# A two-layer diffusion trunk on one core: the modulation vectors are summed, biased and stored in another way, and their background steps are placed at other points

## The chip, the cores and the metric

The kernel runs on 1 core of one Trainium2 chip. The metric is the device time of the whole program in microseconds (us). The kernel before ran three times: 1853.0, 1855.58 and 1855.71 us, median 1855.58 us. The one execution that the profiler recorded took 1847.79 us.

## The reference, cut to what matters

The model has two layers over 512 latent tokens and 256 context tokens, each 1024 wide, in float32. Layer 0 mixes tokens by neighbourhood attention beside a spatial gating unit, layer 1 by a retention mixer. Each layer ends with a gated MLP that holds a depthwise convolution. Six modulation vectors per layer, the adaLN vectors, shift, scale and gate every sub-layer:

```python
silu_c = jax.nn.silu(c)
silu_cc = jax.nn.silu(c_ctx)
for i in range(DEPTH):                      # DEPTH = 2
    ctx_out = i < DEPTH - 1
    mod_lat = (silu_c @ ada_w[i] + ada_b[i])[:, None, :]
    mod_ctx = (silu_cc @ ada_w[i] + ada_b[i])[None, None, :]
    sh1, sc1, g1, sh2, sc2, g2 = jnp.split(mod_lat, 6, axis=-1)
    ...
    h_lat = modulate(rmsnorm(x, norm_g[i, 0]), sh1, sc1)      # x * (1 + scale) + shift
    ...                                                       # hybrid mixer or retention
    x = x + g1 * rmsnorm(y_lat, norm_g[i, 1])
    h = modulate(rmsnorm(x, norm_g[i, 2]), sh2, sc2)
    x = x + g2 * rmsnorm(conv_ffn(h, ...), norm_g[i, 3])
    ...                                                       # the same for the context, in layer 0
```

`ada_w` is 2 x 1024 x 6144 floats, 50 MB. The product with a single row (one for the latent tokens, one for the context) has very little arithmetic for each byte, and the change is about how the kernel computes it beside everything else.

## The kernel before, in words

**Stages.** The program goes through five stages in order: the spatial gating unit (`sgu`, from 0 to about 160 us of the span), the attention heads (`attention`, about 160 to 360, with the residual and norm that follow it to about 430), the MLP of layer 0 (`ffn(0)`, to about 935), the retention mixer (`retention`, to about 1475) and the MLP of layer 1 (`ffn(1)`, to the end). Float32 matmuls are made of three products of a high and a low part each (`mm3`); every weight block of 128 x 1024 floats (512 KB) is loaded by the SP queue into one of three buffers called `raw`, and `split` makes the high part on ACT and the low part on DVE.

**The background job.** Almost all adaLN vectors are computed in the background by `ada_half`, a Python generator. One half is 512 columns of one of the six vectors, so a layer has halves 0 to 11. Layer 0 computes halves 4 to 11 this way for two streams (latent and context), layer 1 halves 0 to 3 for two streams and 4 to 11 for one. For each half, four loads of 512 KB called `ar` go through the same three `raw` buffers as the weights; for each of the eight 128-row blocks and each stream DVE does `acc = raw * c + acc` over 128 x 512 elements, with `c` one scalar for each partition. So `acc` holds 128 partial sums for each column. Then `split` makes `ah` (ACT) and `al` (DVE) of it, and TensorE adds over the partitions: with a matrix of ones (`ag`) for the gate vectors, whose product with the norm weights `ngr` goes to a gate tile, or with a selector (`ac`) for shift and scale, whose result is copied (`arow`), transposed (`at`) and put into small tiles called `ab`. The MLP of layer 0 has no room for its gate in the on-chip memory, so there (`away`) the product goes out to DRAM.

**How the sum starts in the kernel before.** GpSimd (POOL) clears `acc`, and a load puts the bias row into its partition 0, before the eight DVE steps.

**Where the steps stand.** The generator stops at each `yield`. The main program calls `self.bg()` at chosen points, and each call runs the job to its next stop. The calls for the sgu stage stand in its two loops; `attention` has three in the first projection (`project_pair`, which fills `pq`, `px`, `pk`, `pv` and `py` for a pair of heads, from weights `wq`, `wk` and `wv`) and one at every second of its 42 tile steps; `ffn(0)` has two or three and one or two more in each iteration over `j`; `retention` runs four steps after head 0 and four in each later head. A tile step of `attention` does the scores of one tile (`s`, then `sc` on DVE and ACT) and, two steps later, the transposes (`pt`) and the product with the values (`o`). After each pair of heads `take_qk` splits the projections into `q`, `ka` and `kb`, and POOL copies a part of `kb`. In `retention` a head has projections `rk`, `rq`, `rkc`, its `v` and `g` products (`rn`), the output transposes (`rt`) and the output product (`wr`); the weights of head 1 are `rwk1`, `rwq1`, `rwv1` and those of the output `rwo`.

**What sets the order.** A scheduler places the instructions of each engine from its own estimate of their times; an instruction that is issued with `V.hold` on keeps its place in the program's order. Each engine runs its instructions strictly one after the other, and so does each DMA queue: an instruction that waits holds up all that stand behind it. DMAs with an addition (`accum_op`) are issued by POOL, which also issues the DMAs that add the MLP's partial results `yp` to `yd` or `yf` in DRAM.

Of the kernel before, what the change touches and what calls it, by code (L numbers as in the profile page):

```python
# [13 lines left out]
ALU = mybir.AluOpType  # L14
# [64 lines left out]
class Trunk:  # L79
# [171 lines left out]
    def ada_half(self, l, half, streams, gate=None, away=False, fine=False, side=False):  # L251
        S, V, T, G = self.S, self.V, self.T, self.G
        m, h = divmod(half, 2)
        acc = []
        for s in range(streams):
            t = (self.lp if s else self.bp).tile([P, 512], F32, name=f"acc{l}{half}{s}", tag=f"acc{s}", bufs=1)
            G.memset(t, 0.0)
            (G.dma_start if side else self.load)(t[0:1], self.a["adab_row"][l * 12 + half : l * 12 + half + 1])
            acc.append(t)
        for kp in range(4):  # L260
            raw = self.bp.tile([P, 1024], F32, name=f"ar{l}{half}{kp}", tag="raw", bufs=3)
            self.load(raw, self.ada_unit_src(l, half, kp))
            for kk in range(2):
                k = kp * 2 + kk
                for s in range(streams):
                    V.scalar_tensor_tensor(
                        out=acc[s],
                        in0=raw[:, kk * 512 : kk * 512 + 512],
                        scalar=self.cs[:, 8 * s + k : 8 * s + k + 1],
                        in1=acc[s],  # L270
                        op0=ALU.mult,
                        op1=ALU.add,
                    )
                if fine and kk == 0:
                    yield
            yield
        sp = []
        for s in range(streams):
            hi = self.t2k(f"ah{l}{half}{s}", F32R)
            lo = self.t2k(f"al{l}{half}{s}", F32R)  # L280
            self.split(hi, lo, acc[s])
            sp.append((hi, lo))
            if fine:
                yield
            if m in (2, 5):
                ps = self.ps(f"ag{l}{half}{s}", "C")
                T.matmul(ps, self.ones, hi, start=True, stop=False)
                T.matmul(ps, self.ones, lo, start=False, stop=True)
                ngr = self.t2k(f"ngr{l}{half}{s}")
                row = l * 4 + (1 if m == 2 else 3)  # L290
                src = self.a["norm_g"][row : row + 1, h * 512 : h * 512 + 512].broadcast_to([P, 512])
                (G.dma_start if side else self.load)(ngr, src)
                dst = gate[s][:, h * 512 : h * 512 + 512]
                if away:
                    V.tensor_tensor(out=ngr, in0=ps, in1=ngr, op=ALU.mult)
                    G.dma_start(dst, ngr)
                else:
                    V.tensor_tensor(out=dst, in0=ps, in1=ngr, op=ALU.mult)
        if m in (2, 5):
            return  # L300
        ps = self.ps(f"ac{l}{half}", "C")
        n = 2 * streams
        for i in range(n):
            T.matmul(ps[:2], self.sel[:, i // 2, :], sp[i // 2][i % 2], start=(i == 0), stop=(i == n - 1))
        row = self.t2k(f"arow{l}{half}")
        S.copy(row[:2], ps[:2])
        yield
        pt = self.ps(f"at{l}{half}", "C", (P, 4, 2))
        for i in range(4):
            T.transpose(pt[:, i, :], row[:2, i * P : (i + 1) * P], self.ident[:2, :2])  # L310
        ab = self.ab[l, 0 if m < 2 else 1]
        gi = (l * 2 + (0 if m < 2 else 1)) * 8 + h * 4
        for s in range(streams):
            if m in (0, 3):
                V.tensor_copy(ab[:, s, 1, h * 4 : h * 4 + 4], pt[:, :, s])
            else:
                V.scalar_tensor_tensor(
                    out=ab[:, s, 0, h * 4 : h * 4 + 4],
                    in0=pt[:, :, s],
                    scalar=1.0,  # L320
                    in1=self.ng[:, gi : gi + 4],
                    op0=ALU.add,
                    op1=ALU.mult,
                )
# [525 lines left out]
    def attention(self, y, final):  # L850
        a = self.a
        with ExitStack() as ctx:
# [11 lines left out]
            tiles = [(h, b) for h in range(8) for b in (0, 1, 2, 3, 4)]  # L864
            n, lag = len(tiles), 2
            fills = self.project_pair(0, pairs[0])
            for i, f in enumerate(fills):
                f()
                if i in (0, 2, 4):
                    self.bg()  # L870
            self.take_qk(0, pairs[0])
            fills = self.project_pair(1, pairs[1])
            toks = (4, 5, 0, 1, 2, 3)
            for i in range(n + lag):
                if i < n:
                    h, b = tiles[i]
                    j, step = divmod(i, 10)
                    pr = pairs[j]
                    if step == 0:
                        pr["at"] = [ap.tile([P, 768], F32R, name=f"at{x}{j}", tag=f"at{x}", bufs=4) for x in range(2)]  # L880
                        if j == 3:
                            A = (
                                [pairs[0]["at"], pairs[1]["at"]],
                                [self.unit(a["hyb_out"][f * P : (f + 1) * P], f"woa{f}", at=Q3) for f in (0, 1)],
                            )
                            fills = self.out_pieces(*A, y, toks[:1], False, None, "ata", "A")
                    if b == 0:
                        self.bias_tiles(h, heads[h])
                    self.score(h, b, pr, heads[h])
                if fills and i < n:  # L890
                    fills.pop(0)()
                if i < n and step == 7 and j < 3:
                    while fills:
                        fills.pop(0)()
                    self.take_qk(j + 1, pairs[j + 1])
                if i < n and step == 9 and j < 2:
                    fills = self.project_pair(j + 2, pairs[j + 2])
                if i >= lag:
                    h2, b2 = tiles[i - lag]
                    self.weigh(h2, b2, pairs[h2 // 2], heads[h2])  # L900
                if i < n and step == 3:
                    self.take_v(j, pr)
                if i % 2:
                    self.bg()
            self.bg_all()
            for f in fills:
                f()
# [199 lines left out]
    def retention(self, y, final):  # L1107
        S, V, T, G, a = self.S, self.V, self.T, self.G, self.a
        KS = float(np.float32(P) ** np.float32(-0.5))
        with ExitStack() as ctx:  # L1110
# [135 lines left out]
            def score(h, c):  # L1246
                d = hd[h]
                ps = self.ps(f"rs{h}{c}", "B", (P, 2, 256))
                sd = self.t2k(f"sd{h}{c}", shape=(P, 2, 256))
                for i in range(2):  # L1250
                    kt = slice((2 * c + i) * P, (2 * c + i + 1) * P)
                    self.mm3(ps[:, i], [x[:, kt] for x in d["k"]], [x[:, 256 * c : 256 * c + 256] for x in d["q"]], True, True)
                for i in range(2):
                    dm = d["dl"][:, 128 - i * P : 384 - i * P]
                    V.tensor_tensor(out=sd[:, i], in0=ps[:, i], in1=dm, op=ALU.mult)
                s2 = d[c] = [rp.tile([P, 2, 256], F32R, name=f"sd{i}{h}{c}", tag=f"sd{i}", bufs=2) for i in range(2)]
                self.split(s2[0], s2[1], sd)
# [84 lines left out]
            for h in range(8):  # L1342
                vg_tiles(h)
                if h == 0:
                    x = [rp.tile([P, 1024], F32R, name=f"wx{i}", tag=f"kd{i}", bufs=1) for i in range(2)]
                    wv = [w8(self.ready[f"rwv0{i}"]) for i in range(2)]
                    wk = self.ready["rwk0"]
# [12 lines left out]
                    for half in range(2):  # L1360
# [6 lines left out]
                        for n in (range(4) if half else (2, 0, 1, 3)):  # L1367
# [10 lines left out]
                            if half and n == 2:  # L1378
# [1 line left out]
                                score(h, 0)  # L1380
                                score(h, 1)
                                states(h)
                    V.hold = True
                    self.bg(4)
                    V.hold = False
                else:
                    psk = self.ps(f"rk{h}", "A")
                    self.proj_t(psk, wk, 0)
# [13 lines left out]
                    for tp in (2, 0, 1):  # L1402
                        nat(h, wv, tp, "v")
                        if tp < 2:
                            score(h, tp)
                    self.bg()
                    wg = vg(h, 16, "g")
                    states(h)
                    for tp in range(2):
                        nat(h, wg, tp, "g")  # L1410
                    self.bg()
                if h < 7:
                    wk = qk(h + 1, 8, "k")
                else:
                    self.turn += 3
                    o6 = f, w_out(6)
                    self.bg_all()
# [13 lines left out]
    def ffn(self, l, y, final, gates=None):  # L1431
# [13 lines left out]
        with ExitStack() as ctx:  # L1445
# [241 lines left out]
            def o(i):  # L1687
                for _ in range(per[i]):
                    if pieces:
                        pieces.pop(0)()  # L1690
# [4 lines left out]
            for j in range(2, NF):  # L1695
# [20 lines left out]
                meet(pre, 0, 0, Z, ALU.add)  # L1716
                step()
                o(1)
                if j % 2 == 0 and group < LAST:
                    wo = nwo + [w_out(group + 1)]  # L1720
                    pieces += out_steps(feats, wo, group)
# [13 lines left out]
                o(3)  # L1735
                gs[j] = conv(j, pre)
                if j > 3:
                    self.bg(2 if first and j > 5 and j % 2 else 1)
            while pieces:
                o(0)  # L1740
            self.bg_all()
# [225 lines left out]
```

## Time and profile before

| what | before |
|---|---|
| median of three runs | 1855.58 us |
| the profiled execution | 1847.79 us, of which the span of the instructions is 1845.9 us |
| TensorE (PE) busy | 1777.3 us, 96% of the span |
| VectorE (DVE) busy | 1398.2 us, 76% |
| ScalarE (ACT) busy | 1030.1 us, 56% |
| GpSimd (POOL) busy | 331.1 us, 18% |
| the DVE steps of the background sums | 256 instructions, 185.3 us |

PE is the engine that is nearly always busy, so time is gained or lost where PE waits. A row of the waits names the waiting engine and tile and what it waited for, with the total, the number of times and the longest. A row of the timeline has start, length, engine, line, operation, tiles and number of instructions; brackets show how long the engine had been idle before it and what ended that. A row of the windows has the stretch, its length, and for each engine its busy time with its number of instructions, then the mean granted TensorE clock (1.00 is full speed), the share of time that the DMA engines were busy, and GB/s. Nearly all instructions carry one line number (L71, a helper that records them), so the tiles' names tell what an instruction is.

### The profile page before, as it was taken

To read this page: it belongs to the slowest core of one execution; us is meant where nothing else is said; L and a number is where in the kernel's file an instruction comes from. 1 tells how busy PE (TensorE), PEld (TensorE's weight loads), DVE (VectorE), ACT (ScalarE), POOL (GpSimd) and SP (SyncE) were. 2 spreads that over 40 slices of the span, in tenths; PEclk is the share of its full clock that TensorE was granted. 3 is DMA by queue.
4 is the path that set the end of the run, shared out by engine and by line. 5 is a ranking of instruction groups with operands and counts; after the bars stand their busy time and mean duration, and the time that the engine had idled before them with its cause. 6 is when DMAs were issued, how large, how long until landed. Compare 5 with 4: busy or idle time off the path is not lost. (4 is left out here: it accounts for less than half of the span.)

```text
span 1845.9 us, 28788 instructions
## 1 busy us (share of the span) xinstructions
PE 1777.3 (96%) x10928; PEld 1579.5 (86%) x10928; DVE 1398.2 (76%) x2359; ACT 1030.1 (56%) x1866; POOL 331.1 (18%) x462
## 2 busy tenths in 40 slices
PE   7999899999999999999999999999999889999997
PEld 4888777679998899998788989988999789999996
DVE  4877775789878788788867676676556699998887
ACT  6533555677565565565664534344334477766763
POOL 1102122131122322222112011011101100222221
PEclk9999999999999999999999999999999989999999
DMA  8344321155577777787622422331321225887762
GB/s 297 113 141 143 117 86 41 46 179 149 172 153 169 174 182 158 157 173 166 249 97 92 143 98 81 126 106 58 112 69 58 94 83 160 220 204 196 172 161 97
DMA packets 84399, 253.45 MB, mean 137 GB/s; under 512 B 11026, under 2 KB 11538, under 8 KB 84260
## 3 DMA queue, kind: packets, MB, share of 16 engines
q1 hardware_dynamic: 55044, 191.27, 31.3%
q0 software_dynamic: 26912, 51.95, 16.4%
q10 hardware_dynamic: 2304, 8.39, 1.1%
q8 instruction: 86, 1.41, 0.3%
q14 instruction: 53, 0.43, 0.1%
HBM read 191.80 MB, written 39.85 MB: 125 GB/s over the span
## 5 line engine op out<-in xcount | busy, mean ns | idle before, releaser
L71 DVE SCALAR_TENSOR_TENSOR acc<-ar,cs,acc 128x512 f32<-128x512 f32 x256 | 185.3, 749 | 29.4 <-DMA ar<-in_adaw 19.8
L71 DVE SCALAR_TENSOR_TENSOR cv<-pre,cw,cv 128x769 f32<-128x769 f32 (+1 forms) x176 | 153.2, 881 | 5.3 <-ACT cv L71 4.8
L71 PE MATMUL rn<-rwv,h0c 128*128 128x256 f32 x768 | 136.2, 281 | 2.9 <-ACT h0c L71 2.9
L71 PEld LDWEIGHTS rn<-rwv,h0c 128*128 128x128 f32 x768 | 118.1, 191 | 3.6 <-ACT h0c L71 3.3
L71 PE MATMUL wf<-fo,g 128*128 128x512 f32 x432 | 112.4, 394 | 0.1
L71 PE MATMUL rn<-rwv,h1c 128*128 128x256 f32 x384 | 108.1, 282 | 0.4 <-DVE h1c L71 0.2
L1680 POOL DMA_DIRECT2D yf<-yp x64 | 55.1, 861 | 254.4 <-ACT yp L71 231.1
L71 ACT ACTIVATE cv<-pre,cw 128x770 f32<-128x770 f32 (+1 forms) x88 | 81.3, 925 | 22.2 <-DVE pre L71 21.6
L71 PE MATMUL rn<-rwg,h0c 128*128 128x256 f32 x512 | 89.8, 279 | 0.0
L71 PEld LDWEIGHTS wf<-fo,g 128*128 128x128 f32 x432 | 76.0, 188 | 13.0 <-DVE fo L71 0.5
L71 PE MATMUL px<-hs,wc 128*128 128x384 f32 (+1 forms) x480 | 78.4, 311 | 5.1 <-ACT pre L71 2.7
L71 PEld LDWEIGHTS px<-hs,wc 128*128 128x128 f32 x480 | 73.8, 190 | 10.1 <-ACT pre L71 4.3
L71 ACT COPY yp<-wf 128x512 f32<-128x512 f32 x118 | 67.8, 576 | 21.6 <-PE wf L71 18.5
L71 ACT ACTIVATE pre<-px 128x256 f32<-128x256 f32 (+2 forms) x160 | 54.2, 366 | 44.2 <-PE px L71 44.0
L71 PEld LDWEIGHTS rn<-rwg,h0c 128*128 128x128 f32 x512 | 78.0, 189 | 0.0
L71 PE MATMUL pz<-hb,wa 128*128 128x384 f32 (+1 forms) x480 | 77.4, 308 | 0.0
L71 PE MATMUL px<-hb,wa 128*128 128x384 f32 (+1 forms) x480 | 77.2, 308 | 0.0
L71 PE MATMUL py<-blk,wb 128*128 128x384 f32 (+1 forms) x480 | 76.9, 308 | 0.0
L71 PE MATMUL px<-blk,wb 128*128 128x384 f32 (+1 forms) x480 | 76.7, 308 | 0.0
L71 PEld LDWEIGHTS px<-hb,wa 128*128 128x128 f32 x480 | 73.3, 188 | 3.2
L71 PEld LDWEIGHTS px<-blk,wb 128*128 128x128 f32 x480 | 73.2, 188 | 3.0 <-ACT pre L71 0.2
L71 PEld LDWEIGHTS rn<-rwv,h1c 128*128 128x128 f32 x384 | 72.8, 190 | 1.5 <-DVE h1c L71 1.4
(1279 smaller groups left out, 5113.6 us busy)
## 6 DMA issues: line engine op xcount, KB each, us to landing
ar<-in_adaw SPq DMA_DIRECT2D x96, 512.0 KB, 3.9
yf<-yp POOLq DMA_DIRECT2D x64, 256.0 KB, 4.4
yd<-yp POOLq DMA_DIRECT2D x54, 256.0 KB, 4.9
yd<-ypg POOLq DMA_DIRECT2D x54, 256.0 KB, 4.9
fin<-xd SPq DMA_DIRECT2D x8, 512.0 KB
xn<-in_x SPq DMA_DIRECT2D x6, 512.0 KB, 4.9
xb<-in_x SPq DMA_DIRECT2D x6, 512.0 KB
xd<-xb ACTq DMA_DIRECT2D x6, 512.0 KB, 3.1
```

What stands on the lines that cost most here:

```text
L71: i = f(*args, **kw)
L1680: G.dma_start((yd[t] if first else y[t])[:, o], v, accum_op=ALU.add)
```

## The change

The sums no longer start from a cleared tile: the first DVE step writes `raw * c` (one `tensor_scalar`), and the seven others add as before. The bias row is added to partition 0 by an accumulating DMA of POOL's queue, issued after the last step of the sum. In the MLP of layer 0 the gate product is written into the tile of the sum, and goes to DRAM from there. The generator stops at one more place, after the last stream's split (for the gates after each stream's). The calls of `bg` stand elsewhere: none in the first projection of `attention` and then four in five tile steps from the fourth on, with the DVE order held; in `ffn(0)` four in each iteration; in `retention` the weight `rwk1` is asked for ahead of the steps after head 0, of which there are two and not four, and later heads have one step more.

```diff
@@ ada_half
         for s in range(streams):
             t = (self.lp if s else self.bp).tile([P, 512], F32, name=f"acc{l}{half}{s}", tag=f"acc{s}", bufs=1)
-            G.memset(t, 0.0)
-            (G.dma_start if side else self.load)(t[0:1], self.a["adab_row"][l * 12 + half : l * 12 + half + 1])
             acc.append(t)
...
                 for s in range(streams):
-                    V.scalar_tensor_tensor(
-                        out=acc[s],
-                        in0=raw[:, kk * 512 : kk * 512 + 512],
-                        scalar=self.cs[:, 8 * s + k : 8 * s + k + 1],
-                        in1=acc[s],
-                        op0=ALU.mult,
-                        op1=ALU.add,
-                    )
+                    w, c = raw[:, kk * 512 : kk * 512 + 512], self.cs[:, 8 * s + k : 8 * s + k + 1]
+                    if k == 0:
+                        V.tensor_scalar(out=acc[s], in0=w, scalar1=c, scalar2=None, op0=ALU.mult)
+                    else:
+                        V.scalar_tensor_tensor(out=acc[s], in0=w, scalar=c, in1=acc[s], op0=ALU.mult, op1=ALU.add)
                 if fine and kk == 0:
                     yield
+            if kp == 3:
+                for s in range(streams):
+                    row = self.a["adab_row"][l * 12 + half : l * 12 + half + 1]
+                    G.dma_start(acc[s][0:1], row, accum_op=ALU.add)
             yield
...
             self.split(hi, lo, acc[s])
             sp.append((hi, lo))
-            if fine:
+            if fine or m in (2, 5) or s == streams - 1:
                 yield
...
                 if away:
-                    V.tensor_tensor(out=ngr, in0=ps, in1=ngr, op=ALU.mult)
-                    G.dma_start(dst, ngr)
+                    V.tensor_tensor(out=acc[s], in0=ps, in1=ngr, op=ALU.mult)
+                    G.dma_start(dst, acc[s])
@@ attention
             fills = self.project_pair(0, pairs[0])
-            for i, f in enumerate(fills):
+            for f in fills:
                 f()
-                if i in (0, 2, 4):
-                    self.bg()
...
-                if i % 2:
+                if i > 2 and i % 5 != 2:
+                    self.V.hold = True
                     self.bg()
+                    self.V.hold = False
@@ retention, head 0
-                    V.hold = True
-                    self.bg(4)
-                    V.hold = False
+                    wk = qk(1, 8, "k")
+                    self.bg(2)
@@ retention, later heads
                         if tp < 2:
                             score(h, tp)
+                        if tp < 1:
+                            self.bg()
                     self.bg()
...
-                if h < 7:
+                if 0 < h < 7:
                     wk = qk(h + 1, 8, "k")
-                else:
+                elif h:
@@ ffn
                 o(1)
+                if first and j > 3:
+                    self.bg()
...
                 if j > 3:
-                    self.bg(2 if first and j > 5 and j % 2 else 1)
+                    self.bg()
```

## The prediction

> **What bounds the kernel now.** I read the busy times first, then the windows by stage, then the waits of PE, and last the timeline at the two places where the order of the background steps changes most. The page:
>
> ```profile
> PE 1777.3 (96%) x10928; PEld 1579.5 (86%) x10928; DVE 1398.2 (76%) x2359; ACT 1030.1 (56%) x1866; POOL 331.1 (18%) x462
> ...
> L71 DVE SCALAR_TENSOR_TENSOR acc<-ar,cs,acc 128x512 f32<-128x512 f32 x256 | 185.3, 749 | 29.4 <-DMA ar<-in_adaw 19.8
> ...
> ar<-in_adaw SPq DMA_DIRECT2D x96, 512.0 KB, 3.9
> ```
>
> PE is busy for 96% of 1845.9 us, so at most 68.6 us can be had without less PE work, and this change takes none away. The windows say where PE stands still:
>
> ```profile
> core 0: us, PE busy (x) PEld busy (x) DVE busy (x) ACT busy (x) POOL busy (x), PEclk, DMA share, GB/s
> ...
> 160.00:205.00 45.00, 38.90 (x217) 33.57 (x217) 31.59 (x51) 16.34 (x31) 15.73 (x17) 0.92 0.50 154
> 205.00:350.00 145.00, 143.53 (x831) 109.75 (x830) 101.30 (x293) 90.85 (x216) 31.17 (x46) 1.00 0.19 60
> ...
> 438.00:850.00 412.00, 406.88 (x2121) 375.84 (x2121) 336.25 (x478) 239.66 (x413) 99.81 (x130) 1.00 0.72 166
> 850.00:905.00 55.00, 50.12 (x262) 44.88 (x261) 49.90 (x72) 33.86 (x56) 5.74 (x7) 1.00 0.77 239
> ...
> 985.00:1030.00 45.00, 39.60 (x224) 33.08 (x223) 33.41 (x59) 22.60 (x34) 10.15 (x9) 1.00 0.41 138
> 1030.00:1450.00 420.00, 416.53 (x2958) 384.82 (x2958) 264.54 (x465) 175.11 (x251) 40.02 (x56) 1.00 0.28 93
> ```
>
> Idle of PE: 6.1 us in 160 to 205 (45.00 less 38.90, at a granted clock of 0.92), 1.5 in 205 to 350, 5.1 in 438 to 850, 4.9 in 850 to 905, 5.4 in 985 to 1030, 3.5 in 1030 to 1450. So there is something to win in three short windows, and in the attention loop (205 to 350) next to nothing to win and much to lose. The waits of PE over the first stretch and over 850 to 1080:
>
> ```profile
> PE s L71 <- POOL kb L962: 6.1, 1, 6.1
> ```
>
> ```profile
> PE rkc L71 <- ACT rwk L71: 2.1, 1, 2.1
> PE at L71 <- ACT arow L71: 2.0, 1, 2.0
> PE rt L71 <- DVE rg L71: 1.9, 2, 1.6
> PE wf0A L71 <- DVE fin L71: 1.7, 1, 1.7
> ...
> PE ag L71 <- ACT ah L71: 1.1, 1, 1.1
> ```
>
> **The operations themselves.** Of the 256 DVE steps, 32 become `tensor_scalar`.
>
> ```profile
> L71 DVE TENSOR_SCALAR sc<-sc,sst 128x512 f32<-128x512 f32 x30 | 15.0, 499 | 0.7
> ...
> L71 DVE CUSTOM_DVE_ANT_0 sc<-s,tm 128x256 f32<-128x256 f32 x30 | 12.6, 420 | 18.1 <-PE s L71 17.9
> L71 DVE SCALAR_TENSOR_TENSOR acc<-ar,cs,acc 128x512 f32<-128x512 f32 x17 | 12.5, 758 | 0.1
> ...
> L71 DVE RECIPROCAL sst<-sst 128x1 f32<-128x1 f32 x30 | 4.8, 161 | 9.3 <-ACT sc L71 8.8
> ...
> L71 DVE TENSOR_TENSOR at<-o,at 64x512 fp32r<-64x512 f32 x7 | 4.8, 683 | 5.5 <-ACT at L71 5.5
> ```
>
> DVE saves 32 x (749 - 499 ns) = 8.0 us. I put them at nothing: DVE is busy for 76%, and PE covers it; only where DVE is nearly full (attention, below) do they count, and they are in that term.
>
> ```profile
> L257 POOL MEMSET acc<- x32: 524/527/983, 0.9 to 1617.3; 128x512 f32 x32
> L71 ACT ACTIVATE ah<-acc x32: 614/632/640, 94.6 to 1677.2; 128x512 fp32r<-128x512 f32 x32
> ...
> L97 SPq DMA_DIRECT2D acc<-in_adab_row x18: 228/244/303, 51.9 to 1309.5; - x18
> L258 POOL DMA_DIRECT2D acc<-in_adab_row x14: 504/526/850, 282.1 to 1618.1; - x14
> ```
>
> POOL loses 32 x 0.53 = 16.9 us of clearing and gains 18 issues of 0.53 us; at 18% busy neither is on the path. SP loses 18 issues of 0.24 us: nothing. The gate product written to the tile of the sum has the same shape on the same engine: nothing. What is new is that `ah` on ACT can start only when the row DMA has landed behind the last DVE step. Before, the row landed long before:
>
> ```profile
> DMA to landing us min/median/max: 1.7/3.3/6.3
> ```
>
> So between the last step of a sum and its split stand 0.5 us of issue and 1.7 to 6.3 us of landing. POOL waits too, for the last step: behind it on POOL stand the `kb` copies and table loads in attention and the `yd` additions in the MLP. Price from both sides: nothing where the program gives the split later than that (retention, where the split stands some 45 us behind), and up to 6.8 us of ACT for each split where it follows at once. The price is part of the terms by stage.
>
> **160 to 205 us.** The timeline, DVE and then PE:
>
> ```profile
> 168.83 5.79 DVE L71 SCALAR_TENSOR_TENSOR acc<-ar,cs,acc 128x512 f32<-128x512 f32 x8
> ...
> 187.42 0.75 DVE L71 SCALAR_TENSOR_TENSOR acc<-ar,cs,acc 128x512 f32<-128x512 f32 x1 [5.20 <-DMA ar<-in_adaw]
> 188.20 0.42 DVE L71 TENSOR_TENSOR kb<-px,ka 64x256 fp32r<-64x256 f32 x1
> ```
>
> ```profile
> 191.56 0.63 PE L71 MATMUL pq<-h0a,wq 128*128 128x512 f32 x1
> ...
> 198.05 0.28 PE L71 MATMUL s<-ka,q 128*128 128x256 f32 x1
> ```
>
> ```profile
> 1075.47 5.48 PE rq L71 x24
> ```
>
> DVE stands for 5.20 us before a background step whose load is late; the `kb` split stands behind it, POOL copies it, PE waits 6.1 us. In the order of the changed kernel no background step stands there. The first scores then wait for nothing that I can see. Behind the stall the 24 `pq` matmuls take 6.49 us (198.05 less 191.56); 24 matmuls of that kind in retention take 5.48: about 0.9 us, from -0.1 to -3.1 (the whole window at 0.92), goes with the stall. Term: -6.1 - 0.9 = -7.0.
>
> **Attention, the weights of the last pair.** Halves 6 to 9 move some 50 to 80 us later, into the loop. All of `ar` and the weights share three buffers, on SP's queue. The weight `wq3r` takes the buffer of the second `ar` load of half 8, so it waits for the last DVE step on that.
>
> ```profile
> 245.76 0.35 SPq L97 DMA_DIRECT2D wq3r<-in_hyb_qkv  x1
> ```
>
> ```profile
> 276.70 0.68 DVE L71 TENSOR_TENSOR at<-o,at 64x512 fp32r<-64x512 f32 x1 [0.78 <-ACT at L71]
> ```
>
> ```profile
> 279.65 1.09 PE L71 MATMUL pt<-ident,sc 128*128 128x128 f32 x8
> ```
>
> ```profile
> L71 ACT ACTIVATE wq<-wq3r x1: 1059/1059/1059, 249.4 to 249.4; 128x1024 fp32r<-128x1024 f32 x1
> L71 DVE TENSOR_TENSOR wq<-wq3r,wq x1: 1222/1222/1222, 254.5 to 254.5; 128x1024 fp32r<-128x1024 f32 x1
> ```
>
> That step and three before it now stand right behind the DVE row at 276.70: 277.4 + 4 x 0.75 = 280.4. The load lands 3.9 later (284.3), ACT has the high part at 285.4, DVE the low part at 286.6. PE reaches `pq` of this pair behind the `pt` matmuls, at 280.7: a stall of 4.7 us (high part only) to 5.9 (both); I take the middle, 5.3, and 0.8 of clock as after the stall of 6.1. Bounds 0 (the DVE step runs earlier than it stood in time) to 8. The three other weights behind it on SP are asked for in turn, and come in the shadow of this stall. Term: +6.1.
>
> **Attention, the rest of 205 to 350.** DVE gets 52 steps of the sum where it had 17: 35 x 0.758 = 26.5, with two more splits 1.4, less four `tensor_scalar` 1.0: 101.3 becomes 128 of 145 us. The rows above show 18.1 + 9.3 + 5.5 = 32.9 us in which DVE waits in the softmax chain for PE and ACT. The steps stand with held order, so they fill such a wait only where they happen to stand. If u of the 32.9 stay unfilled, the window takes 128 + u. With the four splits waiting on ACT for row DMAs (ACT is at 63%) I take u = 20: +3; bounds 0 and +16. Without them moving, nothing would change here.
>
> **The MLP of layer 0.** Halves 10, 11 and the gates run 17 to 58 us earlier. In 438 to 850 PE idles only 5.1 us of 412, and one split can hold ACT for one landing: +1 (-2 to +4). In 850 to 905 the background is over before the stage's end; `at` (2.0) and a part of the wait for `fin` (1.7), whose load stands behind `ar` loads, go: -2.5 (-4 to 0).
>
> **Retention.** `rwk1r` is asked for ahead of the next half's loads, some 40 us earlier:
>
> ```profile
> 990.86 4.39 DMA rwk1r<-in_ret_qk
> ```
>
> It arrived at 995.3 and PE waited 2.1 for it; with `rt` (1.9) and `ag` (1.1) I take 5.0 of the 5.4 idle us as gone (0 to -5.4). Later heads have their halves 23 to 35 us later: -0.5 of 3.5.
> In the sgu stage no bias row is loaded ahead of its weights: -1.0 (-2 to +1). MLP of layer 1: nothing.
>
> **The sum.** -7.0 + 6.1 + 3 + 1 - 2.5 - 5.0 - 0.5 - 1.0 = -5.9. The profiled execution took 1847.79 us, so the changed kernel would take 1841.9 beside it. The median of the runs is 1855.58, 7.8 above that execution, so on its scale 1849.7, which I round to 1849.5. Its own range is 1842 to 1852.
>
> **The rivals.**
> 1. *The pair of weights comes in time and the loop hides the rest:* the terms +6.1 and +3 go, -15.0, 1840.6. For it: PE's idle there is 1.5 us, and DVE steps may run ahead of where they stood. Against it: one queue and three buffers.
> 2. *The late windows do not give:* with only the first stall gone, -7.0 + 6.1 + 3 + 1 = +3.1, 1858.7. A wait that ends is taken by the next (`rg`, `fin`), which have other causes than the background job. No change that can be measured, 0.2% being 3.7 us.
> 3. *DVE becomes the bound in the attention loop,* slower: held order leaves the 32.9 us unfilled, so the window takes 161 and not 145: +16 in place of +3, sum +7.1, 1862.7. It decides from u = 26 on, where the sum is 0. For it: PE cannot run on without `sc`, and every step between costs 0.75 us. Against it: tile steps run two ahead.
> 4. *ACT waits for the accumulating DMA,* slower: eight splits in the loop at 3.3 to 6.3 us, 26 to 50, of which half on the path: 19 in the middle in place of 3, sum +10.1, 1865.7. It decides from a landing of 2.2 us on if each is waited for in full. Against it: ACT has 54 us free here, and the split mostly stands some steps behind the DMA.
> The Trainium skill speaks against the change here. "SBUF — State Buffer", section "A bandwidth-pool intuition that's wrong (but worth ruling out)", has a GpSimd DMA at some 620 ns alone and 3100 ns beside a DVE copy that holds the shared port, since GpSimd then cannot write descriptors; as an estimate, eight times 3.1 is 25 us on ACT, half of it 12.4, and the sum would be +3.5. "DMA: Bandwidth & Descriptors" of the Trainium skill, section "Anatomy of one DMA — SWDGE (gpsimd) path", puts about 2.0 us on each such DMA: an estimate of 16 us, half of it 8, and the sum -0.9. The median landing of 3.3 us lies near the first, the least of 1.7 below the second; no row here tells which DVE instruction ran beside a landing.
>
> **How the numbers follow.** Forecast 0.43, rival 1 0.10 (both faster), rival 2 0.15 (same), rival 3 0.20, rival 4 0.12 (slower): 0.53, 0.15, 0.32. The range goes from 1839 to 1864, which leaves out about half of rivals 1, 3 and 4, 0.2 in all.
>
> **What would show it.** Right: no wait of `s` for `kb` near 185; `kb` split at once; a PE wait of about 5 us at the first `pq` of the last pair; no wait of `rkc` for `rwk`. Wrong: waits of PE for `sc` or `ptall` that sum to over 10 us between 205 and 350 (rival 3); ACT idle behind the row's landing ahead of `ah` over 3 us in most of 32 splits (rival 4); a new wait after `fin` or `rg` of the same length (rival 2). The prediction fails most easily if the held steps stand at the wrong place in the softmax chain.

## The result, and the profile after

The changed kernel took 1876.44 us (median of four runs, 1872.28 to 1877.65) against 1855.22 us before on the same chip: the ratio is 1.0117, with a 95% interval of 1.0103 to 1.0130, so it is 21 us slower. The forecast was 1849.5 us, 6 us faster. Its profiled execution took 1877.65 us.

The page of the changed kernel, busy times and the group of the background's sums:

```profile
PE 1791.7 (96%) x10928; PEld 1587.9 (85%) x10928; DVE 1389.4 (74%) x2359; ACT 1028.2 (55%) x1866; POOL 336.7 (18%) x448
...
L71 DVE SCALAR_TENSOR_TENSOR acc<-ar,cs,acc 128x512 f32<-128x512 f32 x224 | 161.9, 751 | 25.7 <-DMA ar<-in_adaw 24.9
```

DVE lost 8.8 us of work (1398.2 before), as the 32 cheaper first steps promised, and the program did not get shorter: PE's share of the span is again 96%, of a longer span. The windows of the changed kernel follow, with the columns of the prediction's windows. From the third row on, the bounds are shifted so that each holds about the same PE work as before; the first is the same stretch of time and holds more of it (262 matmuls for 217), the second a little less (811 for 831):

```profile
160.00:205.00 45.00, 45.00 (x262) 39.49 (x261) 17.91 (x39) 18.85 (x36) 13.51 (x18) 1.00 0.27 89
205.00:372.00 167.00, 149.60 (x811) 111.08 (x811) 124.36 (x324) 92.17 (x215) 43.63 (x47) 0.96 0.25 77
...
460.00:885.00 425.00, 413.26 (x2130) 378.82 (x2129) 344.69 (x498) 244.78 (x423) 99.05 (x122) 0.99 0.72 166
885.00:935.00 50.00, 48.46 (x252) 43.33 (x251) 38.54 (x53) 28.41 (x48) 5.25 (x6) 1.00 0.74 219
...
1015.00:1056.00 41.00, 40.76 (x240) 35.09 (x239) 27.04 (x49) 21.86 (x35) 6.73 (x9) 1.00 0.26 82
1056.00:1477.00 421.00, 417.40 (x2953) 386.30 (x2953) 263.95 (x469) 170.31 (x247) 41.39 (x56) 1.00 0.29 93
```

The stall at 184 is gone (PE is busy for all 45 us), the idle time around 1000 is gone (41 us where 45 were needed), and what is won there is lost twice over in two places: the attention loop, where PE now idles 17 us at a clock of 0.96, and the MLP of layer 0, where it idles 12 in place of 5.

To put numbers on the stages, each matmul of the changed kernel was paired with the same matmul of before (same tiles, same count) and the growth of its delay was read off over each stage. The column "again" is a second profile of the kernel before, taken on another chip, paired in the same way: it shows how far one program drifts.

| stage, in times of before | forecast | changed kernel | before, again |
|---|---|---|---|
| 0 to 180, gating unit and first projection | -1.0 | +3.0 | +1.6 |
| 180 to 205 | -7.0 | -9.1 | +2.4 |
| 205 to 350, attention loop | +9.1 | +27.8 | +0.1 |
| 350 to 440 | 0 | 0 | 0 |
| 440 to 850, MLP of layer 0 | +1 | +12.7 | -1.3 |
| 850 to 905, its end | -2.5 | -4.9 | +4.8 |
| 905 to 1030, retention, first heads | -5.0 | -4.7 | +2.3 |
| 1030 to 1450, later heads | -0.5 | +1.6 | +2.6 |
| 1450 to the end | 0 | +2.4 | +2.6 |

The columns of the two profiles add up to 29 and 15 us. The two profiled executions are 29.9 us apart (1877.65 and 1847.79); the one of before lies 7.4 below its median and the one of the changed kernel 1.2 above, which leaves the measured 21. Single values under some 5 us count only where they recur.

### The profile page after: what moved, and what is told of

Read it like the earlier page. It is cut to its first block, busy times and chain, and to the rows that moved or that the text cites. A ratio compares the mean times of both kernels' runs of the same rounds, so it can differ in the third digit from the quotient of the medians.

```text
span 1875.6 us, 28757 instructions
## 1 busy us (share of the span) xinstructions
PE 1791.7 (96%) x10928; PEld 1587.9 (85%) x10928; DVE 1389.4 (74%) x2359; ACT 1028.2 (55%) x1866; POOL 336.7 (18%) x448
## 5 line engine op out<-in xcount | busy, mean ns | idle before, releaser
L71 DVE SCALAR_TENSOR_TENSOR acc<-ar,cs,acc 128x512 f32<-128x512 f32 x224 | 161.9, 751 | 25.7 <-DMA ar<-in_adaw 24.9
```

The source lines that it names most:

```text
L71: i = f(*args, **kw)
```

## The experiments

Two theories stood at first. A: what costs is the accumulating DMA, since ACT, and DVE and PE behind it, wait for its landing. B: what costs is the new placement. Ratios are to runs of the kernel before on the same chip, with 95% intervals.

**One part undone or done alone.** The first run keeps all placements and puts the old start of the sums back.

```diff
+            G.memset(t, 0.0)
+            (G.dma_start if side else self.load)(t[0:1], self.a["adab_row"][...])
...
-                    if k == 0:
-                        V.tensor_scalar(out=acc[s], in0=w, scalar1=c, scalar2=None, op0=ALU.mult)
...
-                    G.dma_start(acc[s][0:1], row, accum_op=ALU.add)
```

> The changed kernel with one part undone: every sum starts again from a cleared tile with the bias row loaded ahead of it; all placements stay new. Theory A (the accumulating DMA: ACT stands behind its landing ahead of ah, and DVE and PE behind ACT): ACT's nine waits of 18.4 us go, the stall of PE at 214 us (4.9) with its 3.4 of clock goes, so about 1876 - 14 = 1862. Theory B (the placement alone: the three buffers and the held DVE order in attention): at most 3 us, 1873 to 1877, with the stalls of PE at 214 and at 284 unchanged.

Measured: 1.0046 (1.0027 to 1.0066), 8.6 us slower than before, so 13 us of the 21 go with the old start, near theory A's forecast. The second run does the reverse: the kernel before with only the new start (`tensor_scalar` and the accumulating DMA in, clearing and early row load out).

> The kernel before with one part of the change: the sums start with a scaled copy and the bias row comes by the accumulating DMA; the gates, the stops and all placements stay as before. Theory A: ACT waits at ah in the first projection and in the attention loop, 8 to 15 us slower than before, 1863 to 1870. Theory B: 1855 to 1858.

Measured: 1.0017 (0.9997 to 1.0036). With the old placements the new start costs 3 us, not clear of none, which was theory B's forecast. So neither part explains the loss alone; the two do it together. Where it costs, the timeline of the changed kernel shows; first at 97 us, in the gating unit:

```profile
96.96 1.82 POOL L274 DMA_DIRECT2D acc<-in_adab_row  x2 [8.78 <-DVE acc L71]
...
101.31 1.30 ACT L71 ACTIVATE ah<-acc 128x512 fp32r<-128x512 f32 x2 [4.23 <-DMA acc<-in_adab_row]
...
101.97 0.69 DVE L71 TENSOR_TENSOR al<-acc,ah 128x512 fp32r<-128x512 f32 x1 [4.66 <-ACT ah L71]
...
102.93 0.47 PE L71 MATMUL mx<-vnh,sguw 128*128 128x384 f32 x1 [1.86 <-ACT un L71]
```

ACT stands 4.23 us for the landing, and the activation `un` that PE needs stands behind it. By 160 to 180 us the three kernels with the new start and the old calls in the first projection (this one and two below) are 8.0 to 9.1 us late, the second profile of before 1.6. Then in the attention loop, at 214:

```profile
207.21 0.63 POOL L982 DMA_DIRECT2D slab<-in_rpb  x1 [0.30 <-POOL tm L996]
211.59 0.40 POOL L989 TENSOR_SCALAR slab<-slab 128x256 f32<-128x256 f32 x1 [3.75 <-DMA slab<-in_rpb]
212.11 1.68 POOL L274 DMA_DIRECT2D acc<-in_adab_row  x2
...
214.23 0.63 ACT L71 ACTIVATE ah<-acc 128x512 fp32r<-128x512 f32 x1 [2.81 <-DMA acc<-in_adab_row]
...
214.90 0.69 DVE L71 TENSOR_TENSOR al<-acc,ah 128x512 fp32r<-128x512 f32 x1 [2.50 <-ACT ah L71]
...
219.74 1.97 PE L71 MATMUL o<-ptall,vn 128*64 128x512 f32 x2 [4.92 <-ACT ptall L71]
```

The last step of the sum ended on DVE at 208.8, but the row DMA is issued only at 212.1: POOL stood 3.75 us for a table load ahead of it. Then come the landing, the ACT split, and behind that split, with other work of ACT between, the copy `ptall` that PE waits for. A wait on one queue became a wait on three engines. Over the whole of the changed kernel there are nine such waits of ACT, 18.4 us in all:

```profile
ACT ah L71 <- DMA acc<-in_adab_row: 18.4, 9, 4.2
```

**The attention placement.** The changed kernel with the old calls there:

```diff
-                if i > 2 and i % 5 != 2:
-                    self.V.hold = True
-                    self.bg()
-                    self.V.hold = False
+                if i % 2:
+                    self.bg()
```
(and the three calls in the first projection, and no added stop for these halves).

> The changed kernel with the attention placement (calls, held order, the new stop for these halves) as before; the start of the sums and the other placements stay new. Theory B: the stall of s for kb at 184 comes back (+8.5), those at 214 (8.3), at 284 to 292 (11.3) and around 330 (6.5) go: 1876 - 18 = 1858. Theory A: the accumulating DMA costs as much at the old places, some 1868.

Measured: 1.0044 (1.0028 to 1.0059), 8.2 us slower than before, between the two forecasts. The loop from 205 to 350 is as short as before and the stall at 184 is back, so the placement loses 13 us on balance. Next, the stall that the prediction had worked out, at 284 in the changed kernel:

```profile
282.91 0.33 SPq L97 DMA_DIRECT2D wq3r<-in_hyb_qkv  x1
...
286.45 1.06 ACT L71 ACTIVATE wq<-wq3r 128x1024 fp32r<-128x1024 f32 x1 [1.58 <-DMA wq3r<-in_hyb_qkv]
...
287.56 0.80 PE L71 MATMUL pq<-h0a,wq 128*128 128x512 f32 x1 [3.63 <-ACT wq L71]
```

Is this queue the bound of the loop (theory C), or DVE and its held order (theory D)? One run lets the weights pass two background loads, the other drops the held order.

```diff
-                if i > 2 and i % 5 != 2:
+                if i > 2 and i % 5 != 2 and not 14 < i < 20:
```

> The changed kernel without the background calls of tile steps 15 to 19, so that the three weights of the last pair are asked for two background loads earlier (the steps left out follow behind the loop). Theory C (three shared buffers on one queue): the wait of pq for wq near 284 (3.6) goes and with it the 8.7 to 11 us that the trace shows between 278 and 292; 10 us faster than the changed kernel, 10 to 12 slower than before. Theory D (DVE is full, with steps held in the softmax chain): the time moves to other waits in the loop, within 3 us of the changed kernel (20 slower than before).

```diff
-                    self.V.hold = True
                     self.bg()
-                    self.V.hold = False
```
(and, as in the run with the old calls above, no added stop for the halves that run up to the end of attention).

> The changed kernel without the held order of the background's DVE steps in the attention loop. Theory D: the scheduler may move the steps into the waits of the softmax chain, 8 us or more faster than the changed kernel. Theory C: the stall near 284 stays, within 3 us of the changed kernel (20 slower than before).

Measured: 1.0146 (1.0126 to 1.0165) for the first, 27 us slower than before, more than the change itself; 1.0049 (1.0030 to 1.0068) for the second, 9 us slower, so dropping the held order together with the added stop gives back 12 us. In the first run the stall at 284 is gone (from 220 to 300 nothing is lost), and some 25 us are lost between 305 and 345, mostly in waits for `sc` and `vt`. The steps left out did not leave the loop: all 52 still stand in it, 16 of them in its last 45 us, where the changed kernel has 7. So the run shows that the weights in time do not make the loop short, and theory C falls as its only bound; but it also crowded the steps at the loop's end, and what the weights alone would have given is not shown.

Is it the held order itself? The kernel before with the held order at its old calls:

```diff
                 if i % 2:
+                    self.V.hold = True
                     self.bg()
+                    self.V.hold = False
```

> The kernel before with one edit: the background's DVE steps in the attention loop keep their place in the program's order, at the old calls (17 steps of the sums there). If held order costs by itself, the loop from 205 to 350 loses 5 us or more against the kernel before. If it costs only with 52 steps in the loop, the loop loses at most 2 us and the time is that of before.

Measured: 0.9986 (0.9969 to 1.0003), the same time as before. The loop lost 7 us and the stretch to 205 gained 4. By the forecast that is held order costing by itself; but 28 steps stood in the loop where 17 had, so this run does not separate the order from the number of steps. So I counted, for every kernel, the DVE steps of the sums in the stretch that holds the same PE work (205 to 350 before). Two of these stretches, of the changed kernel and of the one without the held order; first the groups and the window of the changed kernel:

```profile
L71 DVE SCALAR_TENSOR_TENSOR acc<-ar,cs,acc 128x512 f32<-128x512 f32 x46 | 32.9, 763 | 0.0
L71 DVE TENSOR_SCALAR acc<-ar,cs 128x512 f32<-128x512 f32 x6 | 2.6, 477 | 0.0
```

```profile
199.00:372.00 173.00, 155.60 (x850) 116.52 (x850) 125.49 (x329) 93.58 (x218) 45.04 (x48) 0.96 0.24 75
```

and those without the held order:

```profile
L71 DVE SCALAR_TENSOR_TENSOR acc<-ar,cs,acc 128x512 f32<-128x512 f32 x22 | 17.3, 827 | 2.7 <-DMA ar<-in_adaw 2.7
L71 DVE TENSOR_SCALAR acc<-ar,cs 128x512 f32<-128x512 f32 x2 | 1.0, 476 | 0.0
```

```profile
210.00:359.00 149.00, 144.86 (x838) 110.31 (x836) 105.82 (x295) 90.01 (x214) 35.60 (x44) 1.00 0.22 66
```

| kernel | steps in the loop | held | length of the loop, us |
|---|---|---|---|
| new start alone, old calls in attention, the two kept parts (below), before again | 16 | no | 145 |
| before | 17 | no | 145 |
| one call less in the projection (below) | 20 | no | 147 |
| two calls less (below) | 24 | no | 150 |
| the change without held order | 24 | no | 149 |
| the same with the old start (below) | 27 | no | 153 |
| before with held order | 28 | yes | 152 |
| the change with the old start | 52 | yes | 165 |
| the change | 52 | yes | 173 |
| the change with the gap | 52 | yes | 177 |

The length goes with the number of steps, with the flag or without it: 27 steps without it make 153 us, 28 with it 152. No run changes the flag and keeps the number. From 17 to 52 steps with the old start the loop grows by 20 / 35 = 0.57 us for each, against 0.75 us that a step lasts. The window of that kernel, the change with the old start, shows it best, since no accumulating DMA stands in it:

```profile
192.00:357.00 165.00, 151.80 (x851) 114.78 (x850) 128.90 (x328) 93.12 (x218) 40.20 (x50) 0.98 0.26 78
```

DVE has 27.6 us more work than before (128.90 for 101.30), and the loop is 20 us longer. Before, DVE had 43.7 us without work in the loop; only 7.6 of them were filled, 36.1 are left, and DVE is busy for 78%. PE's waits for `sc` sum to 7.5 us there (the longest 3.9), and no step waits for a load. In the changed kernel DVE is busy for 125.49 of 173 us, 73%: it is not full, and yet the steps lengthen the loop.

For the kernels without held order the number of steps is not the whole cause. Much of what they lose falls at one place near 210, where DVE stands before a step whose load is late, as in the stall at 184. The kernel with 27 steps:

```profile
204.89 1.41 DVE L71 SCALAR_TENSOR_TENSOR acc<-ar,cs,acc 128x512 f32<-128x512 f32 x2 [2.13 <-DMA ar<-in_adaw]
```

```profile
210.03 0.69 PE L71 MATMUL vn<-ident,vt 128*128 128x128 f32 x2 [4.41 <-ACT ptall L71]
```

By 220 it has lost 6.6 of its 8 us; with two calls less it is 3.9 of 5. What these rows would lose without the late load is not shown.

So the change costs what it does in the loop because 52 steps stand there; without held order (and without the added stop) the scheduler leaves 24 and puts the others ahead. The accumulating DMA adds 8 us to that (173 against 165).

**The MLP of layer 0.** In every kernel with the new calls the stretch from 440 to 850 loses 10.5 to 13.2 us, whatever the start of the sums (13.2 with the old start). With the old calls it loses less than 1, or gains 3 with the new start. Two theories. E: too many steps in an iteration. F: the added step stands ahead of the request for the output weights `fo` on SP's queue; ACT's waits for `fo` sum to 12 us in the changed kernel and 6 before. One run puts the second step at the end of each iteration, in a kernel with the retention part and the new start kept (see below), the other moves the step behind the request for `fo`, in the changed kernel with the old attention.

```diff
-                    self.bg(2 if first and j > 5 and j % 2 else 1)
+                    self.bg(2 if first else 1)
```

> The same two kept parts, old attention, and in the MLP of layer 0 two steps at the end of every iteration from j = 4 on (before: two only in odd iterations from j = 7): as many steps in each iteration as the change has, but none ahead of the request for the output weights fo. Theory E (too many steps in an iteration: DVE and ACT are late for the convolution): the MLP of layer 0 loses 8 to 13 us between 440 and 850, so 3 to 8 slower than before. Theory F (the added step asks for its 512 KB ahead of fo on SP's queue, so fo lands late): at most 3 us lost there, 3 to 6 faster than before.

```diff
                 o(1)
-                if first and j > 3:
-                    self.bg()
...
                 o(2)
                 if j % 2 and j - 1 < LAST:
                     nwo = [w_out(j - 1)]
                 if first and j > 3:
-                    self.bg()
+                    self.bg(2)
```

> The changed kernel with the old attention placement (8.2 us slower than before in its run) and one more edit: the step added in each iteration of the MLP of layer 0 is called after the request for fo and not ahead of it, so that the same number of steps stands in each iteration. Theory F: ACT's waits for fo (some 12 us) and with them 6 to 10 of the 10.5 us between 440 and 850 go; equal to before within 3 us. Theory E: nothing changes, 8 us slower than before.

Measured: 1.0003 (0.9989 to 1.0018) for the first, 0.6 us slower than before and 6 slower than the same kernel without the edit; its stretch from 440 to 850 loses 11.4. 1.0066 (1.0041 to 1.0091) for the second, 12 us slower than before; its stretch loses 12.3. The total of the first lies between the two forecasts, its stretch in that of E. The waits for `fo` sum to 9.2 us in the first, against 7.1 in the same kernel without the edit: 2 us more, while the stretch loses 14 more. So late `fo` loads do not carry the loss, and theory F falls. The second run did not do what it was made for: its waits for `fo` did not go (13.7 us), so it only shows that the place of the step does not matter. E is what is left, the number of steps in an iteration, wherever they stand; it fits the waits of PE, but no run shows it apart from the loads that each step brings along. The window of the first of the two runs and its waits of PE, the like of which the changed kernel has:

```profile
440.00:863.00 423.00, 411.36 (x2129) 377.97 (x2128) 344.53 (x498) 245.02 (x422) 99.41 (x122) 1.00 0.73 167
```

```profile
PE wf L71 <- ACT ypg L71: 3.5, 2, 2.6
PE px L71 <- ACT pre L71: 2.8, 2, 2.4
PE px L71 <- DVE pre L71: 2.4, 1, 2.4
PE wf L71 <- ACT yp L71: 1.4, 1, 1.4
```

PE idles 11.6 us there, in the waits for the convolution's inputs (`pre`) and for the copies of its results. Only 7 more steps of the sums stand in this stretch than before (96 against 89), with one split more; most of the other DVE instructions that the window counts more are the MLP's own, at its edges. DVE has 8.3 us more work and the stretch is 11.4 longer, so the price is over their own length. Part of it comes back: with the background done earlier, the stretch 850 to 905 gains 5.

**Retention, and the parts worth keeping.** The kernel before with the retention placement alone:

```diff
-                    V.hold = True
-                    self.bg(4)
-                    V.hold = False
+                    wk = qk(1, 8, "k")
+                    self.bg(2)
```
(with one step more in each later head and the added stop).

> The kernel before with the retention part alone (rwk1 asked for ahead, two steps and one more in later heads, the new stop for these halves). If the gain of 5 us that the two traces show between 975 and 1020 belongs to this part: 1850. If it was idle time that the later start of the stage freed: 1855, with rkc waiting for rwk as before.

Measured: 0.9998 (0.9981 to 1.0014): no gain at the end. In the trace the stretch 980 to 1090 gains 5.3, as it does in every kernel with this placement (4.8 to 6.5), and 8 are lost between 1250 and 1350. Of these, 3 near 1340 come and go in kernels with and without the placement, the second profile of before among them; 4.7 near 1270, in waits of `rt` for `rg`, are in this kernel alone, and their cause was not settled. The next run adds the new start, only for the halves beside the MLP of layer 0 and beside retention, and keeps all else as before.

> The kernel before with two parts of the change: the retention placement, and the new start of the sums (scaled copy, accumulating DMA) only for the halves that run beside the MLP of layer 0 and beside retention. By the four runs so far, stage by stage: MLP of layer 0 -3, retention -5, elsewhere 0: 8 us faster than before. The rival is that the loss of 8.5 us between 1260 and 1345, seen with the new retention placement and the old start, belongs to that placement: then no faster than before.

Measured: 0.9970 (0.9955 to 0.9986), 5.6 us faster than before, in the trace 3.2 in the MLP of layer 0 and 5.3 in 980 to 1090, with some 5 lost near 1340. These two parts are worth keeping. On top of them one call less in the first projection:

```diff
-                if i in (0, 2, 4):
+                if i in (0, 2):
```

> The kernel with the two kept parts (retention placement; new start of the sums only beside the MLP of layer 0 and retention) and one call of the background less in the first projection of attention (the third of three; its step falls to the next call). If the stall of s for kb near 184 comes from the background step whose load is late, it goes or shrinks: 4 to 8 us faster than the kernel without this edit, 10 to 14 faster than before. If the step merely comes again at the next call, the stall stays: 5.6 faster than before, as without the edit.

Measured: 0.9951 (0.9932 to 0.9970), 9 us faster than before, the lowest ratio of this study and a little less than forecast; the interval overlaps that of the kernel without this edit. Its wait at 184:

```profile
PE s L71 <- POOL kb L964: 2.0, 1, 2.0
```

2.0 us are left of 6.1. With two calls less (`if i == 0:`):

> The two kept parts with two calls less in the first projection of attention (before had three). If the rest of the stall of s for kb near 184 (2.0 us with one call less) goes and the loop still hides the steps: 1 to 3 us faster than with one call less, 10 to 12 faster than before. If the steps that move into the loop push DVE there as in the change: 5 us or more lost in the loop, 3 to 6 faster than before.

Measured: 0.9971 (0.9954 to 0.9987), 5.4 us faster than before. In the trace the wait shrinks to 0.7 and the loop takes 150 us and not 147; the difference to one call less lies within both intervals. That is the second of the two outcomes. The change's attention calls, without the held order and with the old start, on the same base:

> The two kept parts with the change's attention placement, but without the held order and with the old start in these stages; old placement in the MLP of layer 0. If the held order and the accumulating DMA are what the attention placement costs, it keeps its gains (some 5 us in the first projection and 7 at 184) and loses 2 to 4 in the loop: 10 to 15 us faster than before. If the placement itself costs (DVE at 88%): no faster than the kernel with the two kept parts, 5 faster than before.

Measured: 0.9965 (0.9953 to 0.9978), 6.5 us faster than before. It gains 8 by 205 and gives 8 back in the loop (153 us), 6.6 of them behind the late load shown above. So the placement itself costs what it gains here.

**Before, a second time.** This run is the column "again" above; the time of this one run was 1862.7 us, beside a median of 1859.11 there.

> The kernel before itself, for a second profile. If two profiles of one program agree in every stage to 1 us, the differences of one stage between kernels can be read from single profiles; if they drift by several us, only those that recur in several kernels count.

Its profile drifts from the first by up to 4.8 us in a stage, at single waits (190, 860 to 880, 1010, 1340, 1660); the attention loop and the MLP of layer 0 agree within 1.3.

## Why the prediction was wrong, step by step

- **160 to 205 us, -7.0: right in mechanism and size.** No wait of `s` for `kb` is left, the stretch gained 9.1.
- **The weights of the last pair, +6.1: right in its place, but not shown to be a term by itself.** `wq3r` was asked for at 282.91 (forecast 280.4 in times of before; PE was 2.9 late there), and PE waited 3.63 us at the `pq` matmuls, where 4.7 to 5.9 were forecast. The run with the gap removed this stall and was no faster, with more steps at the loop's end.
- **Attention, the rest, +3: this is the step that failed.** I took 32.9 us of DVE waits in the softmax chain as room that added steps could fill, with 20 of them left over. With 52 steps and the old start, DVE still had 36.1 us without work: of 27.6 us of added work 7.6 found room, and the loop grew by 20. The loop also got four more splits (8 for 4), where the term counted two. That was rival 3, priced at +16 for the loop where the runs give 20 with the old start, 28 with the new. Its sign was not quite met: PE's waits for `sc` and `ptall` in the loop sum to 7.9 us in the changed kernel, where over 10 were asked for.
- **The accumulating DMA, "part of the terms by stage": too small.** Rival 4 came true in part, together with rival 3 and not to the size of its sign (ACT waits for the landing at nine splits, over 3 us at three of them). The landing from which it was to decide, 2.2 us, is right for half of each wait; for whole waits, as written there, it is 1.1. The runs show 8 us in the loop, and 6.4 to 7.5 in the gating unit, where I had forecast -1.0 because I looked only at the queue of SP and not at ACT behind the landing. The emptied first projection hid part of it (+3.0 in the table). The rivals were priced as alternatives; both happened.
- **The MLP of layer 0, +1: wrong, the second step that failed.** It lost 12.7. I read 5.1 us of PE's idle time as slack and counted no price for denser steps in a stage where DVE was busy for 82% (336.25 of 412). The end of the stage gained more than forecast (-4.9 for -2.5).
- **Retention, -5.0: right in its place** (-4.7, and -5.3 where it was done alone); in the run of this part alone the end did not come earlier, and why is open.
- **The first steps by `tensor_scalar`, nothing: right.** DVE saved 8.8 us, and no stage shows a gain from it alone. With the old calls the MLP of layer 0 gains 3 us with the new start; which part of the new start does that was not tried.

By the profiles the changed kernel is 29 us late where -5.9 was forecast, a difference of 34.9. Three steps carry it: 18.7 in the loop (27.8 for 9.1), 11.7 in the MLP and 4.0 up to 180 us.

## What to carry to other kernels

Idle time of an engine inside a dependent chain (scores, maximum, exponential, sum, transposes, one tile after the other) was not room here: count the length of the chain before and after, not the engine's busy share, and see how many instructions are pinned into the loop. Here the load that a sum needs was cheaper at its start, where nothing waited for it, than at its end, where ACT stood for its landing (13 of the 21 us); if it must come last, look at what stands ahead of it on its queue and behind the waiter on that one's engine. Of a change made of many moves, keep those whose stage shows a gain, undo the rest, and measure again: here that turned a loss of 1.2% into a gain of 0.5%.

## What the runs showed of the hardware that was not expected

The tile of the sums in the changed kernel, its row DMAs and then their landing:

```profile
L274 POOL DMA_DIRECT2D acc<-in_adab_row x32: 757/847/1240, 97.0 to 1702.5; - x32
```

```profile
DMA to landing us min/median/max: 2.0/3.8/6.8
```

For a row of 2 KB the accumulating DMA takes 0.85 us of POOL to issue, where the plain one took 0.53, and lands in a median of 3.8 us for 3.3. The Trainium skill, "DMA: Bandwidth & Descriptors", section "Anatomy of one DMA — SWDGE (gpsimd) path", has about 2.0 us fixed for such a DMA: here that is the least of 32, not the middle; no run separated what the rest is.

The granted clock of the loop was 0.96 in the changed kernel, with stalls of PE of 4.92 and 3.63 us, and 1.00 before, with 0.7 at most. The Trainium skill, "TensorE: Matmul & The Clock Gate", section "Part 1: The HAM clock gate", has the clock halved after an idle window of about 3.4 us; the two stalls agree. In the MLP of the changed kernel the clock was halved too, at 0.51 from 584.5 to 588.0 and at 0.50 from 669.8 to 673.2, beside waits of PE of 2.52 and 2.37 us, which are shorter than that; there the measurement does not go with the page's figure. The same DVE step lasted 0.75 us on the mean before in the loop, and 0.89 in the loop with held order at the old calls (28 steps); why was not tried.
